# RWKV-7 layer: head sums for two blocks at a time in parts of the array's columns, low LoRA products paired over the two halves of rows

## The chip, the cores and the metric

The kernel runs on one core of one Trainium2 chip. The metric is the device time of one execution in microseconds (us). The engines are named as in the profile: PE (TensorE, matrix products; PEld is its loading of weights), DVE (VectorE), ACT (ScalarE), POOL (GpSimd) and SP (which issues most DMAs).

## The reference

A decoder trunk of two layers over 512 tokens with 1024 features, all in fp32: a recurrent RG-LRU block, then an RWKV-7 time mixing block, each followed by a gated MLP with a convolution. The change touches the RWKV-7 block only, which has 16 heads of 64 features. What matters of it:

```python
w = -jax.nn.softplus(-(w0 + jnp.tanh(xw @ w1) @ w2).astype(f32)) - 0.5      # LoRA, rank 64
decay = jnp.exp(-jnp.exp(w))
a = jax.nn.sigmoid((a0 + (xa @ a1) @ a2).astype(f32))                        # LoRA, rank 64
kk = (kf * k_k).reshape(bsz, seq, RWKV_H, RWKV_N)
kk = kk / jnp.maximum(jnp.linalg.norm(kk, axis=-1, keepdims=True), 1e-12)    # sum of squares of each head
kf = kf * (1.0 + (a - 1.0) * k_a)
y = _rwkv7_scan(rh, hs(decay), kh, vh, -kk, kk * ah)                         # recurrence over the tokens
...
bonus = jnp.sum(rh * kh * r_k, axis=-1, keepdims=True) * vh                  # a weighted sum over each head
y = (y + bonus.reshape(bsz, seq, d)).astype(x.dtype)
```

## The kernel before

**Layout and products.** Activations lie with features on the 128 partitions, in 8 blocks of 128 features by 512 tokens; a block holds two heads. A large fp32 product is made of three products of type fp32r (`mm3`, lines 51 to 53): each operand is split into a rounded part (hi) and the rest (lo), and hi x hi, lo x hi and hi x lo are summed in PSUM. PSUM has 8 banks of 128 x 512, taken with `self.bank(name)`. Products of plain fp32 tiles, such as those of lines 915 and 1294, stand in the trace as two instructions a call.

**Order of the work.** Side work is written as Python generators. `push(task, lane)` puts one in a lane, and the large projections (`project`) call `background(rate)` after every six matmuls, which advances the generators by that many `yield` steps. The framework then orders each engine's instructions, in the main by program order and by when they are ready in its own model of time, and it chooses tile buffers and semaphores; on the chip each engine takes its instructions in that fixed order.

**Stages of the RWKV-7 block** (times from the start of the profiled execution's span).

- `rwkv_lora_k`, about 586 to 617: the first half of the k projection; beside it the generator `second` makes, block by block, the decay's and a's second LoRA products. A rank-64 operand is kept as 128 rows, hi in one half and lo in the other, so that hi x (hi and lo) is one product over 128 rows (lines 840 and 848), and the lo of the weights needs a second one over 64 rows (line 841 on rows 0 to 63, line 849 on rows 64 to 127). A sigmoid on ACT follows each (843 and 850), and four scans on DVE (846) the decay's.
- `rwkv_krv`, about 617 to 700: the second half of k, and r. Beside it `prepare(g)` runs for g = 0 and 1, each over four blocks j: ACT makes exponentials and squares (`sq`, tag "tmp", two buffers), and PE sums the squares over each head with the selector `sel` into 8 rows of one bank, `ssq` (line 915, accumulated over j). After the fourth, ACT copies the 8 rows (926), PE turns them by four transposes (930) so that tokens lie on partitions, DVE takes reciprocals (932 to 934), PE turns them back (938) and spreads them over the features again (947). Then `solve(H)` (lane 1, later 2) inverts small triangular blocks: PE products (1017), 31 pairs of DVE operations (1038 and 1040), DVE transposes (1043 and 1045), PE products (1062 and 1074).
- `rwkv_chunks`, from about 700: v by tokens (lines 986 to 988), then the recurrence in 17 steps of one 64-token chunk each (`step(n)`: L1198, L1206, L1150, L1216, L1164, L1229, L1243 on PE; L1157, L1179, L1237 and L1238 on DVE), with other generators as filling. `bonus(H)`, H = 0 and 1, is one of these: DVE makes a product `pr` for each of four blocks (line 1292, tag "sq", three buffers that are shared with `ysq` and `bv` of `tail`), PE sums it over heads with the selector `selk`, which holds r_k (line 1294, accumulated into 8 rows), ACT copies (1296), PE transposes (1300), ACT copies to `bons[H]` (1301). `tail(H, c2)` normalises the output of two chunks and needs `bons[H]`; its last transposes are line 1275.

`tile_position=(row, column)` on a matmul names the corner of the part of the 128 x 128 array that it uses. The recurrence uses it throughout.

Of the kernel before, what the change touches and what calls it, by code (L numbers as in the profile page):

```python
# [7 lines left out]
F32 = mybir.dt.float32  # L8
F32R = mybir.dt.float32r
AF = mybir.ActivationFunctionType  # L10
ALU = mybir.AluOpType
# [4 lines left out]
P = 128  # L16
D = 1024
T = 512
KB = D // P
# [22 lines left out]
class Kernel:  # L42
# [647 lines left out]
    def rwkv(self):  # L690
        nc, tc = self.nc, self.tc
        x = self.x
        with tc.tile_pool(name="rbig", bufs=1) as big:

            PC = big.tile([P, KB, NC], F32, name="PC")
            selk = big.tile([P, KB, 8], F32, name="selk")

            early = [big.tile([P, 2, 2, T], F32R, tag=f"LT{i}", name=f"early{i}", bufs=1) for i in range(2)]
            again = lambda name, *shape, dt=F32: big.tile([P] + list(shape), dt, tag=name, name=name, bufs=1)
            self.LT, self.big = lambda i: again(f"LT{i}", 32, C), big  # L700

            with tc.tile_pool(name="rl", bufs=1) as pool:
                AR, BK = ([again(f"{part}{i}", 4, 4, 4 * C) for i in range(2)] for part in ("AR", "BK"))
                mk, mr = self.rwkv_lora_k(pool, AR, BK, early)
            LTs = {}
            with tc.tile_pool(name="rk", bufs=1) as pool:
                mv = self.rwkv_krv(pool, mk, mr, AR, BK, PC, selk, LTs)
            with tc.tile_pool(name="rch", bufs=1) as pool:
                return self.rwkv_chunks(pool, mv, AR, BK, PC, selk, LTs, again)
# [31 lines left out]
    @staticmethod  # L741
    def bytok(t):
        return t.rearrange("p (c q t) -> p c q t", q=2, t=C)
# [34 lines left out]
    def rwkv_lora_k(self, pool, AR, BK, early):  # L778

        nc, I = self.nc, self.I  # L780
# [13 lines left out]
        tw, ta = pool.tile([P, T], F32R, name="tw"), pool.tile([P, T], F32R, name="ta")  # L794
# [24 lines left out]
        def second():  # L819

            keep = pool.tile([P, 2, C], F32, name="keep")
            nc.vector.memset(keep, 1.0)
            nc.vector.memset(keep[:, :, 0:1], 0.0)
            kp = keep.rearrange("p q t -> p (q t)")
            ws = []
            for name, r in (("w2", 0), ("a2", 64)):
                raw = self.b4(F32, (D,), "l2raw")
                nc.sync.dma_start(raw[0:64, :], I["rwkv_" + name][0])
                nc.sync.dma_start(raw[64:128, :], I["rwkv_" + name][0])
                hi, lo = self.b4(F32R, (D,), "l2h"), self.b4(F32R, (D,), "l2l")  # L830
                nc.scalar.copy(hi, raw)
                nc.vector.tensor_tensor(lo[r : r + 64, :], raw[r : r + 64, :], hi[r : r + 64, :].bitcast(F32), ALU.subtract)
                ws.append((hi, lo))
                yield 1
            for _ in range(3):
                yield 1
            for b in range(KB):
                s = slice(b * P, (b + 1) * P)
                ps = self.bank("l2w")
                nc.tensor.matmul(ps, ws[0][0][:, s], tw, start=True, stop=False)  # L840
                nc.tensor.matmul(ps, ws[0][1][0:64, s], tw[0:64, :], start=False, stop=True)
                sg = pool.tile([P, T], F32, tag="sg", name="sg", bufs=2)
                nc.scalar.activation(sg, ps, AF.Sigmoid, bias=self.vec("rwkv_w0", b))
                yield 1
                for c in range(4):
                    nc.vector.tensor_tensor_scan(AR[b // 4][:, b % 4, c, C : 3 * C], kp, sg[:, c * P : (c + 1) * P], 0.0, ALU.mult, ALU.add)
                ps = self.bank("l2a")
                nc.tensor.matmul(ps, ws[1][0][:, s], ta, start=True, stop=False)
                nc.tensor.matmul(ps, ws[1][1][64:128, s], ta[64:128, :], start=False, stop=True)
                nc.scalar.activation(self.inner(BK, b), self.bytok(ps), AF.Sigmoid, bias=self.vec("rwkv_a0", b))  # L850
                yield 1

        self.push(second())

        mr = []
# [13 lines left out]
    def rwkv_krv(self, pool, mk, mr, AR, BK, PC, selk, LTs):  # L869

        nc = self.nc

        def t(tag, bufs):
            return pool.tile([P, T], F32, tag=tag, name=tag, bufs=bufs)


        sel = pool.tile([P, 4, 40], F32, name="sel")
        n8 = pool.tile([P, 4, 40], F32, name="n8")
        for m in (sel, selk, n8):
            nc.gpsimd.memset(m, 0.0)  # L880
        for e in range(2):
            hb = slice(e * 64, e * 64 + 64)
            for b in range(4):
                for part in (0, 32):
                    c = part + 2 * b + e
                    nc.gpsimd.memset(sel[hb, b, c : c + 1], 1.0)
            for b in range(KB):
                c = 2 * (b % 4) + e
                nc.gpsimd.tensor_copy(selk[hb, b, c : c + 1], self.vec("rwkv_r_k", b)[hb])
        psb = self.bank("back")  # L890
        for j in range(4):
            nc.tensor.transpose(psb[0:40, j * P : (j + 1) * P], sel[:, j, :], self.ident)
# [7 lines left out]
        def prepare(g):  # L900


            ssq = self.bank("ssq")
            for j in range(4):
                b = g * 4 + j
                pad = ppads[b % 2]
                pp = pad.rearrange("p (c q) t -> p c q t", q=2)
                Lc, rr, a, ko = self.inner(AR, b), self.outer(AR, b), self.inner(BK, b), self.outer(BK, b)
                sq, pinv, fac, kp = t("tmp", 2), t("pinv", 2), t("fac", 1), t("kp", 1)
                nc.scalar.activation(bytok(pinv), Lc, AF.Exp, scale=DECAY_C)  # L910
                nc.scalar.activation(bytok(sq), ko, AF.Square, scale=self.vec("rwkv_k_k", b))
                nc.scalar.activation(bytok(fac), a, AF.Identity, bias=self.oka[:, b : b + 1], scale=self.vec("rwkv_k_a", b))
                nc.scalar.activation(pp[:, :, :, 1:], Lc, AF.Exp, scale=-DECAY_C)
                yield 1
                nc.tensor.matmul(ssq[0:8, :], sel[:, j, 0:8], sq, start=j == 0, stop=j == 3)  # L915
                nc.vector.tensor_tensor(bytok(kp), ko, bytok(pinv), ALU.mult)
                nc.vector.scalar_tensor_tensor(a, a, self.vec("rwkv_k_k", b), bytok(kp), ALU.mult, ALU.mult)
                yield 1
                (nc.vector.tensor_copy if g else nc.scalar.copy)(rr, pp[:, :, :, 1:])
                self.done.add(("r", b))  # L920
                nc.vector.tensor_tensor(Lc, ko, pp[:, :, :, 0:C], ALU.mult)
                nc.vector.tensor_tensor(ko, bytok(kp), bytok(fac), ALU.mult)
                nc.scalar.copy(PC[:, b, :], pad[:, :, C])
                yield 1
            ss = t("tmp", 2)[0:8]
            nc.scalar.copy(ss, ssq[0:8])
            yield 1
            pt = self.bank("sst")
            for c in range(4):
                nc.tensor.transpose(pt[:, c * 8 : c * 8 + 8], ss[:, c * P : (c + 1) * P], self.ident[0:8, 0:8])  # L930
            pv = pt[:, 0:32].rearrange("p (c h) -> p c h", h=8)
            nc.vector.tensor_scalar(n8[:, :, 0:8], pv, 1e-24, None, ALU.max)
            for part in (32, 0):
                nc.vector.reciprocal(n8[:, :, part : part + 8], n8[:, :, 0:8])
            yield 1
            pr = self.bank("rec")
# [6 lines left out]
            for j in range(4):  # L943
                b = g * 4 + j
# [137 lines left out]
    def rwkv_chunks(self, pool, mv, AR, BK, PC, selk, LTs, again):  # L1082
# [9 lines left out]
        nc, tc, I = self.nc, self.tc, self.I  # L1092
# [21 lines left out]
        bons = [pool.tile([P, 4, 8], F32, name=f"bon{i}") for i in range(2)]  # L1114
# [171 lines left out]
        def bonus(H):  # L1286

            pn = self.bank("bon")
            for i in range(4):
                b = H * 4 + i  # L1290
                pr = self.xsp.tile([P, T], F32, tag="sq", name="pr", bufs=3)
                nc.vector.tensor_tensor(self.bytok(pr), self.outer(AR, b), self.outer(BK, b), ALU.mult)
                yield 1
                nc.tensor.matmul(pn[0:8, :], selk[:, b, :], pr, start=i == 0, stop=i == 3)
            bt = self.xsp.tile([P, T], F32, tag="sq", name="bt", bufs=3)
            nc.scalar.copy(bt[0:8, :], pn[0:8, :])
            yield 1
            pt = self.bank("bont")
            for c in range(4):
                nc.tensor.transpose(pt[:, c * 8 : c * 8 + 8], bt[0:8, c * P : (c + 1) * P], self.ident[0:8, 0:8])  # L1300
            nc.scalar.copy(bons[H], pt[:, 0:32].rearrange("p (c h) -> p c h", h=8))
            self.done.add(("bonus", H))
            yield 1

# [199 lines left out]
```

## Time and profile before

| | |
|---|---|
| runs | 1363.87, 1361.54, 1357.82 us; median 1361.54 |
| profiled execution | 1359.88 us, span of its instructions 1357.9 us |
| granted PE clock, mean | 0.989 |
| PE, PEld busy | 1324.4 us, 1068.8 us |
| DVE, ACT, POOL busy | 863.6, 632.6, 68.8 us |
| DMA | 120.20 MB, mean 89 GB/s |

Busy time of PE is the union of its matmuls' durations, whose ends are modelled: matmuls overlap, so the distance between starts tells more of a matmul's cost than its duration does. In the rows, `128*8` is the part of the array (rows by columns) and `128x512` the data that is streamed; "x16" counts instructions. L12 is line 12 of the kernel before. "Idle before" is time in which the engine did nothing ahead of the instruction, with what released it.

### The profile page before, as it was taken

To read this page: it belongs to the slowest core of one execution; us is meant where nothing else is said; L and a number is where in the kernel's file an instruction comes from. 1 tells how busy PE (TensorE), PEld (TensorE's weight loads), DVE (VectorE), ACT (ScalarE), POOL (GpSimd) and SP (SyncE) were. 2 spreads that over 40 slices of the span, in tenths; PEclk is the share of its full clock that TensorE was granted. 3 is DMA by queue.
4 is the path that set the end of the run, shared out by engine and by line. 5 is a ranking of instruction groups with operands and counts; after the bars stand their busy time and mean duration, and the time that the engine had idled before them with its cause. 6 is when DMAs were issued, how large, how long until landed. Compare 5 with 4: busy or idle time off the path is not lost.

```text
span 1357.9 us, 19301 instructions
## 1 busy us (share of the span) xinstructions
PE 1324.4 (98%) x7827; PEld 1068.8 (79%) x7827; DVE 863.6 (64%) x1332; ACT 632.6 (47%) x1032; POOL 68.8 (5%) x113
## 2 busy tenths in 40 slices
PE   8999999999999999999999988898999999999998
PEld 7877888888888888866679776676888888888886
DVE  5988756555354755597897975776646464365623
ACT  6797534333233523378636578653634242244311
POOL 4000000000000000020011011110000000000000
PEclk8999999999999999999999989998999999999999
DMA  5423333232333434222121111212333222334311
GB/s 182 119 62 93 109 94 109 79 104 67 106 94 94 143 93 125 63 72 79 62 86 49 58 33 64 56 60 65 109 93 94 77 93 78 109 94 126 122 63 62
DMA packets 72120, 120.20 MB, mean 89 GB/s; under 512 B 9498, under 2 KB 21476, under 8 KB 71904
## 3 DMA queue, kind: packets, MB, share of 16 engines
q1 hardware_dynamic: 70672, 117.20, 27.9%
q8 instruction: 61, 1.00, 0.3%
q10 hardware_dynamic: 576, 1.05, 0.2%
q0 software_dynamic: 784, 0.74, 0.2%
q14 instruction: 27, 0.22, 0.1%
HBM read 114.44 MB, written 4.52 MB: 88 GB/s over the span
## 4 chain that ended last, share of the span: by engine, by line
PE 89%; DVE 6%; ACT 2%; issue 1%; DMA 1%; POOL 1%; SPq 0%; POOLq 0%; ACTq 0%; DVEq 0%
PE acc L51 22%; PE acc L53 22%; PE acc L52 22%; PE acc L616 3%; PE acc L615 3%; PE acc L617 3%; PE acc L986 1%; PE s L1150 1%; PE pe L1198 1%; PE acc L987 1%; PE py L1206 1%; PE acc L988 1%; DVE W L1157 1%; PE ssq L915 1%; DMA xin<-in_x_dram 1%
## 5 line engine op out<-in xcount | busy, mean ns | idle before, releaser
L51 PE MATMUL acc<-xs,wh 128*128 128x512 f32 x896 | 352.1, 393 | 0.0
L53 PE MATMUL acc<-xs,wl 128*128 128x512 f32 x896 | 349.0, 390 | 0.7 <-DVE wl L91 0.7
L52 PE MATMUL acc<-xs,wh 128*128 128x512 f32 x896 | 349.5, 390 | 0.0
L91 DVE TENSOR_TENSOR wl<-raw,wh 128x1024 fp32r<-128x1024 f32 (+1 forms) x201 | 242.6, 1215 | 164.6 <-PE acc L52 90.1
L90 ACT CAST wh<-raw 128x1024 fp32r<-128x1024 f32 (+1 forms) x201 | 208.1, 1045 | 258.6 <-DVE wl L91 167.6
L53 PEld LDWEIGHTS acc<-xs,wl 128*128 128x128 f32 x896 | 168.5, 188 | 36.5 <-DVE wl L91 1.2
L51 PEld LDWEIGHTS acc<-xs,wh 128*128 128x128 f32 x896 | 168.8, 188 | 35.0 <-ACT wh L90 0.2
L52 PEld LDWEIGHTS acc<-xs,wh 128*128 128x128 f32 x896 | 168.7, 188 | 34.7 <-DVE wl L91 0.2
L576 DVE SCALAR_TENSOR_TENSOR cv<-gpad,pv,cv 128x512 f32<-128x512 f32 x96 | 71.8, 748 | 22.6 <-ACT cv L574 21.5
L90 ACT CAST hid<-un 128x512 fp32r<-128x512 f32 x48 | 29.8, 620 | 109.2 <-DVE un L583 109.1
L616 PE MATMUL acc<-wh,hid 128*128 128x512 f32 (+1 forms) x200 | 76.8, 384 | 0.0
L615 PE MATMUL acc<-wh,hid 128*128 128x512 f32 (+1 forms) x200 | 76.5, 382 | 0.0
L617 PE MATMUL acc<-wl,hid 128*128 128x512 f32 (+1 forms) x200 | 75.9, 380 | 0.0
L52 PE MATMUL acc<-hid,wh 128*128 128x512 f32 x192 | 75.7, 394 | 0.0
L53 PE MATMUL acc<-hid,wl 128*128 128x512 f32 x192 | 75.6, 394 | 0.0
L51 PE MATMUL acc<-hid,wh 128*128 128x512 f32 x192 | 75.5, 393 | 0.0
L582 DVE TENSOR_TENSOR un<-acc,rb 128x512 f32<-128x512 f32 x48 | 33.0, 688 | 43.5 <-PE acc L53 43.5
L91 DVE TENSOR_TENSOR hid<-un,hid 128x512 fp32r<-128x512 f32 x48 | 33.1, 690 | 32.0 <-ACT hid L90 32.0
L574 ACT ACTIVATE cv<-gpad,pv 128x512 f32<-128x512 f32 x48 | 39.2, 817 | 20.1 <-DVE gpad L571 19.9
L578 ACT ACTIVATE ge<-cv 128x512 f32<-128x512 f32 x48 | 30.1, 627 | 35.9 <-DVE cv L576 35.9
L620 DVE TENSOR_TENSOR xtok<-xtok,acc 128x512 f32<-128x512 f32 (+1 forms) x25 | 16.6, 665 | 45.6 <-PE acc L617 45.6
L615 PEld LDWEIGHTS acc<-wh,hid 128*128 128x128 f32 x200 | 37.5, 188 | 8.0
(424 smaller groups left out, 2207.6 us busy)
## 6 DMA issues: line engine op xcount, KB each, us to landing
raw<-in_ffn_w_up_dram SPq DMA_DIRECT2D x96, 512.0 KB, 3.9
raw<-in_ffn_w_down_dram SPq DMA_DIRECT2D x48, 512.0 KB, 3.8
raw<-in_rwkv_w_rkv_dram SPq DMA_DIRECT2D x24, 512.0 KB, 3.8
raw<-in_lru_w_in_dram SPq DMA_DIRECT2D x16, 512.0 KB, 3.9
raw<-in_lru_w_out_dram SPq DMA_DIRECT2D x8, 512.0 KB, 3.7
raw<-in_rwkv_w_out_dram SPq DMA_DIRECT2D x8, 512.0 KB, 3.5
xd<-x SPq DMA_DIRECT2D x8, 256.0 KB, 2.0
AR<-xd SPq DMA_DIRECT2D x1, 2048.0 KB, 8.8
```

What stands on the lines that cost most here:

```text
L51: nc.tensor.matmul(ps, wh, xh, start=start, stop=False)
L52: nc.tensor.matmul(ps, wh, xl, start=False, stop=False)
L53: nc.tensor.matmul(ps, wl, xh, start=False, stop=stop)
L90: (self.nc.vector.tensor_copy if dve else self.nc.scalar.copy)(hi, src)
L91: self.nc.vector.tensor_tensor(lo, src, hi.bitcast(F32), ALU.subtract)
L574: nc.scalar.activation(cv, gp[:, 0:T], AF.Identity, bias=self.vec(f"ffn_conv_b{l}", fb), scale=cw(0))
L576: nc.vector.scalar_tensor_tensor(cv, gp[:, j : j + T], cw(j), cv, ALU.mult, ALU.add)
L578: nc.scalar.activation(ges[o], cv, AF.Gelu_apprx_tanh)
L582: nc.vector.tensor_tensor(un, ps, rbs[0], ALU.mult)
L615: nc.tensor.matmul(ps, hh[:, s], wh[:, k, m], start=kk == 0, stop=False)
L616: nc.tensor.matmul(ps, hl[:, s], wh[:, k, m], start=False, stop=False)
L617: nc.tensor.matmul(ps, hh[:, s], wl[:, k, m], start=False, stop=kk == 7)
```

## The change

1. **Low LoRA products.** In `second`, each block takes two banks, `pw` and `pa`, at once. The two products over 128 rows come first, then, after a `yield`, the two products over 64 rows next to each other, with `tile_position` (0, 0) and (64, 0); both sigmoids and the scans follow them in the same step. The number of steps, products, sigmoids and scans is the same.
2. **Sums of squares.** In `prepare`, the squares of blocks j = 0 and 1 (then 2 and 3) are kept until both are there, and are then summed by two products next to each other, each into 32 rows of the bank at 32 j, `tile_position` (0, 32 j), not accumulated. The selector is the same 32 columns of `sel` for every block. The copy takes 128 rows instead of 8, the transposes are 128 x 128 instead of 8 x 128, and DVE reads columns 0 and 1 of each strip of 32.
3. **Bonus.** The same in `bonus`: two products `pr` are kept, then summed by a pair of products in strips of 32 columns; copy, transposes and the last copy change likewise. `selk` has 32 columns a block instead of 8.

```diff
-            selk = big.tile([P, KB, 8], F32, name="selk")
+            selk = big.tile([P, KB, 32], F32, name="selk")
...
             for b in range(KB):
                 s = slice(b * P, (b + 1) * P)
-                ps = self.bank("l2w")
-                nc.tensor.matmul(ps, ws[0][0][:, s], tw, start=True, stop=False)
-                nc.tensor.matmul(ps, ws[0][1][0:64, s], tw[0:64, :], start=False, stop=True)
+                pw, pa = self.bank("l2w"), self.bank("l2a")
+                nc.tensor.matmul(pw, ws[0][0][:, s], tw, start=True, stop=False)
+                nc.tensor.matmul(pa, ws[1][0][:, s], ta, start=True, stop=False)
+                yield 1
+
+                nc.tensor.matmul(pw, ws[0][1][0:64, s], tw[0:64, :], start=False, stop=True, tile_position=(0, 0))
+                nc.tensor.matmul(pa, ws[1][1][64:128, s], ta[64:128, :], start=False, stop=True, tile_position=(64, 0))
                 sg = pool.tile([P, T], F32, tag="sg", name="sg", bufs=2)
-                nc.scalar.activation(sg, ps, AF.Sigmoid, bias=self.vec("rwkv_w0", b))
-                yield 1
+                nc.scalar.activation(sg, pw, AF.Sigmoid, bias=self.vec("rwkv_w0", b))
                 for c in range(4):
                     nc.vector.tensor_tensor_scan(AR[b // 4][:, b % 4, c, C : 3 * C], kp, sg[:, c * P : (c + 1) * P], 0.0, ALU.mult, ALU.add)
-                ps = self.bank("l2a")
-                nc.tensor.matmul(ps, ws[1][0][:, s], ta, start=True, stop=False)
-                nc.tensor.matmul(ps, ws[1][1][64:128, s], ta[64:128, :], start=False, stop=True)
-                nc.scalar.activation(self.inner(BK, b), self.bytok(ps), AF.Sigmoid, bias=self.vec("rwkv_a0", b))
+                nc.scalar.activation(self.inner(BK, b), self.bytok(pa), AF.Sigmoid, bias=self.vec("rwkv_a0", b))
                 yield 1
...
             for b in range(KB):
-                c = 2 * (b % 4) + e
-                nc.gpsimd.tensor_copy(selk[hb, b, c : c + 1], self.vec("rwkv_r_k", b)[hb])
+                nc.gpsimd.tensor_copy(selk[hb, b, e : e + 1], self.vec("rwkv_r_k", b)[hb])
...
             ssq = self.bank("ssq")
+            sqs = []
...
-                nc.tensor.matmul(ssq[0:8, :], sel[:, j, 0:8], sq, start=j == 0, stop=j == 3)
+                sqs.append(sq)
+                for i in (j - 1, j) if j % 2 else ():
+                    nc.tensor.matmul(ssq[32 * i : 32 * i + 32, :], sel[:, 0, 0:32], sqs[i], start=True, stop=True, tile_position=(0, 32 * i))
...
-            ss = t("tmp", 2)[0:8]
-            nc.scalar.copy(ss, ssq[0:8])
+            ss = t("tmp", 2)
+            nc.scalar.copy(ss, ssq)
             yield 1
             pt = self.bank("sst")
             for c in range(4):
-                nc.tensor.transpose(pt[:, c * 8 : c * 8 + 8], ss[:, c * P : (c + 1) * P], self.ident[0:8, 0:8])
-            pv = pt[:, 0:32].rearrange("p (c h) -> p c h", h=8)
-            nc.vector.tensor_scalar(n8[:, :, 0:8], pv, 1e-24, None, ALU.max)
+                nc.tensor.transpose(pt[:, c * P : (c + 1) * P], ss[:, c * P : (c + 1) * P], self.ident)
+            pv = pt.rearrange("p (c j w) -> p c j w", c=4, w=32)[:, :, :, 0:2]
+            nc.vector.tensor_scalar(n8[:, :, 0:8].rearrange("p c (j e) -> p c j e", e=2), pv, 1e-24, None, ALU.max)
...
             pn = self.bank("bon")
+            prs = []
             for i in range(4):
                 b = H * 4 + i
                 pr = self.xsp.tile([P, T], F32, tag="sq", name="pr", bufs=3)
                 nc.vector.tensor_tensor(self.bytok(pr), self.outer(AR, b), self.outer(BK, b), ALU.mult)
+                prs.append(pr)
                 yield 1
-                nc.tensor.matmul(pn[0:8, :], selk[:, b, :], pr, start=i == 0, stop=i == 3)
+
+                for j in (i - 1, i) if i % 2 else ():
+                    nc.tensor.matmul(pn[32 * j : 32 * j + 32, :], selk[:, H * 4 + j, :], prs[j], start=True, stop=True, tile_position=(0, 32 * j))
             bt = self.xsp.tile([P, T], F32, tag="sq", name="bt", bufs=3)
-            nc.scalar.copy(bt[0:8, :], pn[0:8, :])
+            nc.scalar.copy(bt, pn)
             yield 1
             pt = self.bank("bont")
             for c in range(4):
-                nc.tensor.transpose(pt[:, c * 8 : c * 8 + 8], bt[0:8, c * P : (c + 1) * P], self.ident[0:8, 0:8])
-            nc.scalar.copy(bons[H], pt[:, 0:32].rearrange("p (c h) -> p c h", h=8))
+                nc.tensor.transpose(pt[:, c * P : (c + 1) * P], bt[:, c * P : (c + 1) * P], self.ident)
+            nc.scalar.copy(bons[H].rearrange("p c (j e) -> p c j e", e=2), pt.rearrange("p (c j w) -> p c j w", c=4, w=32)[:, :, :, 0:2])
```

## The prediction, made before the changed kernel was run

> **What bounds the kernel now.** I read the page first, then the busy time by stage, then PE's waits, and then the order of PE's instructions around every line the change touches.
>
> ```profile
> PE 1324.4 (98%) x7827; PEld 1068.8 (79%) x7827; DVE 863.6 (64%) x1332; ACT 632.6 (47%) x1032; POOL 68.8 (5%) x113
> ...
> PE 89%; DVE 6%; ACT 2%; issue 1%; DMA 1%; POOL 1%; SPq 0%; POOLq 0%; ACTq 0%; DVEq 0%
> ```
>
> PE carries 89% of the chain that ended last, so a microsecond of PE time counts wherever PE does not wait. The stages in which the changed lines run (times from the span's start) are these:
>
> ```profile
> core 0: us, PE busy (x) PEld busy (x) DVE busy (x) ACT busy (x) POOL busy (x), PEclk, DMA share, GB/s
> 599.40:617.30 17.90, 17.90 (x59) 9.65 (x57) 13.12 (x34) 12.85 (x20) 0.04 (x1) 1.00 0.34 106
> 617.00:651.00 34.00, 34.00 (x141) 23.38 (x141) 27.46 (x47) 31.86 (x57) 1.04 (x18) 1.00 0.26 78
> 673.60:729.50 55.90, 55.90 (x377) 44.10 (x376) 54.11 (x113) 20.74 (x41) 4.33 (x15) 1.00 0.23 71
> 740.00:786.00 46.00, 42.12 (x623) 34.40 (x622) 43.23 (x101) 29.94 (x72) 5.88 (x5) 1.00 0.18 55
> 786.00:840.00 54.00, 49.49 (x836) 40.21 (x836) 34.47 (x60) 39.17 (x99) 6.60 (x6) 0.91 0.09 27
> ```
>
> In the first three rows PE is busy for the whole stretch. A busy PE may still run with bubbles, which is what this change is about, but it is not waiting for anybody. But the neighbours are close behind: ACT works 31.86 of 34.00 us in the second row, DVE 54.11 of 55.90 us in the third. In the fourth row PE does wait and DVE, at 43.23 of 46.00 us, sets the pace.
>
> **Low LoRA products.** Each of 8 blocks has two of them, over 64 rows of the array (L841, L849). PE start times show what leaving and re-entering the full array costs:
>
> ```profile
> 593.86 0.39 PE L52 MATMUL acc<-mix,wh 128*128 128x512 f32 x1
> 594.08 0.39 PE L53 MATMUL acc<-mix,wl 128*128 128x512 f32 x1
> 594.40 0.49 PE L841 MATMUL l2w<-tw,l2l 64*128 64x512 f32 x1
> 594.82 0.50 PE L51 MATMUL acc<-mix,wh 128*128 128x512 f32 x1
> 595.16 0.40 PE L52 MATMUL acc<-mix,wh 128*128 128x512 f32 x1
> ```
>
> A full matmul starts about 0.23 us after the one before. From L53 (594.08) to the second full one after L841 (595.16) it is 1.08 us where two ordinary steps would be 0.46: one "trip" to a 64-row product costs 0.62 us, though the product alone is worth 0.23. Once the trace already has two such products, on different halves of the rows, side by side:
>
> ```profile
> 600.84 0.39 PE L840 MATMUL l2w<-tw,l2h 128*128 128x512 f32 x1
> 601.15 0.50 PE L849 MATMUL l2a<-ta,l2l 64*128 64x512 f32 x1
> 601.16 0.49 PE L841 MATMUL l2w<-tw,l2l 64*128 64x512 f32 x1
> ...
> 602.15 0.40 PE L848 MATMUL l2a<-ta,l2h 128*128 128x512 f32 x1
> ```
> ```profile
> L841 PE MATMUL l2w<-tw,l2l 64*128 64x512 f32 x8 | 4.0, 495 | 0.0
> L849 PE MATMUL l2a<-ta,l2l 64*128 64x512 f32 x8 | 3.7, 481 | 0.0
> ```
>
> They start 0.01 us apart, so the second is free. That one trip holds three products and takes 602.15 - 600.84 - 0.46 = 0.85 us; the other 13 of the 16 go alone. Before: 13 x 0.62 + 0.85 = 8.9 us. After: eight trips, 5.0 us. I expect block 0 to stay split, because the first L841 runs at 594.40 and the first L849 only at 601.15: 9 trips, 5.6 us, **a gain of 3.3 us**. The ends: 3.9 us gained if all eight pair up, and 16 x 0.62 - 8.9 = 1.0 us lost if none does. I take the upper part, as the two lines now stand next to each other and become ready together.
>
> The full products move ahead of both low ones and hold two banks at once (pw, pa), and the sigmoids, the scan and L850 come in one step. Number, length and engine of those stay; the cover is PE's project matmuls, which go on between the steps. ACT has 5.0 us and DVE 4.8 us left in 599.40 to 617.30, so both fit in a stretch that is 3.3 us shorter; where they don't, a bank comes free late (second rival).
>
> **Sums of squares.** L915 is an fp32 product with 8 columns, and each call runs as two passes (x2):
>
> ```profile
> 625.54 0.39 PE L53 MATMUL acc<-mix,wl 128*128 128x512 f32 x1
> 625.86 1.02 PE L915 MATMUL ssq<-tmp,sel 128*8 128x512 f32 x2
> 626.81 0.50 PE L51 MATMUL acc<-mix,wh 128*128 128x512 f32 x1
> 627.15 0.39 PE L52 MATMUL acc<-mix,wh 128*128 128x512 f32 x1
> ```
> One call costs 627.15 - 625.54 - 0.46 = 1.15 us, eight 9.2 us. After, two calls stand in different 32-column strips and go as a pair. What a pair costs no row shows for 512 columns of data; for 64 there is a close one, fp32 in two passes on the two column halves (L1198):
>
> ```profile
> 744.23 0.68 PE L1198 MATMUL pe<-sv,W 128*64 128x64 f32 x8
> 744.84 0.32 PE L1206 MATMUL py<-sv,rts 64*64 64x64 f32 x2
> ...
> 748.63 1.02 PE L1294 MATMUL bon<-pr,selk 128*8 128x512 f32 x2
> 749.59 0.39 PE L986 MATMUL acc<-wh,mix 128*128 128x256 f32 x1
> ...
> 753.02 0.69 PE L1198 MATMUL pe<-sv,W 128*64 128x64 f32 x16
> 753.63 0.27 PE L1206 MATMUL py<-sv,AR 64*64 64x64 f32 x1
> ```
>
> Eight passes on one half take 0.61 us to the next line (744.23 to 744.84), sixteen on both halves also 0.61 us (753.02 to 753.63): the second half is free. So a pair costs one trip, 1.15 us: four pairs, 4.6 us, **a gain of 4.6 us**. The ends: 4.6, and, with no overlap, two passes more for each pair. Two passes with the exit behind them hold up the follower 0.96 us (748.63 to 749.59); the exit is about what 0.42 (594.40 to 594.82) is over 0.32 (594.08 to 594.40), 0.1, so two passes are 0.86: a gain of 0.29 a pair, 1.2 us in all. I take the upper end, as L1198 is the same kind of pair.
>
> The Trainium skill speaks against this: TensorE: Matmul & The Clock Gate, section "The mechanism", says that a weight load overlaps running matmuls only where its row group differs, and that matmuls start strictly in order; column strips share their rows. L1198's 16 passes in the time of 8 disagree with it so far, at 64 columns of data. What it would give here is the first rival.
>
> Waits that this adds: the pair waits for the later square, so a "tmp" buffer (2 of them) is held one block longer, and the next L911 on ACT can be late. ACT has 2.1 us idle between 617 and 651, so one late square is free there; if more are late, the project's casts of weights behind them on ACT are late too, and the second rival has the price.
>
> **Transposes and copies.** L930 and L1300 become full 128-wide transposes like L938:
>
> ```profile
> L938 PE MATMUL rec<-ident,n 128*40 128x128 f32 x8 | 1.2, 271 | 0.0
> ...
> L930 PE MATMUL sst<-ident,tmp 8*128 8x8 f32 x8 | 0.8, 207 | 0.0
> ```
>
> Sixteen of them at 64 ns more are 1.0 us lost at most; against that each of the four groups need no longer leave the full array (0.62 us a trip above, less if the neighbours are narrow too). Between 1.0 lost and 2.5 gained I take 0.2 us gained, near zero, as both effects are seen in the rows and are of like size. Copies over 128 partitions instead of 8 have the same 512 columns; the larger clearing of selk is on POOL, busy 5%: nothing for both, and if POOL were late the first bonus product, over 100 us later, is the cover.
>
> **Bonus.** The row of L1294 gives its instructions with the first and the last start:
>
> ```profile
> L1294 PE MATMUL bon<-pr,selk x16: 592/594/597, 748.6 to 833.5; 128*8 128x512 f32 x16
> ```
>
> Each call delays its follower 0.96 us, as above. Bonus(0), the first half, lies from 748.6 on in the fourth stage, where DVE sets the pace: the two calls saved (1.9 us) only lengthen PE's next wait, so nothing. Bonus(1), which ends the row, lies in the fifth stage and is partly on the chain; PE is busy 49.49 of 54.00 us there. Two calls saved are 1.9 us at most, 0 at least; I take half, **1.0 us**.
>
> **The sum.** 3.3 + 4.6 + 0.2 + 1.0 = 9.1 us. The profiled execution took 1359.88 us (span 1357.9), so 1350.8 by its measure; it stood 1.66 us under the median of the three runs, 1361.54. For a median I forecast **1352.4 us**.
>
> **Rivals.** *Column strips overlap partly or not.* With no overlap squares give 1.2 and bonus(1) 0.1: 3.3 + 1.2 + 0.2 + 0.1 = 4.8, 1356.7 us, chance 0.05. If the second product's first pass starts only with the first one's second pass, each pair pays half of 0.86: squares 2.9, bonus 0.5, sum 6.9, 1354.6 us, chance 0.07. For both: no row shows 512 columns in strips. Against both: L1198.
>
> The second figure, 1354.6 us, is the one that the Trainium skill's rule on row groups and order, cited above, would give.
>
> *The chain of ACT and DVE is the next bound.* PE's lead must be matched by prepare(0) and the solve.
>
> ```profile
> 727.37 2.08 DVE L1045 STREAM_TRANSPOSE XN<-X 128x1024 f32<-128x1024 f32 x1
> ```
> ```profile
> 731.46 0.69 PE L1062 MATMUL m1p<-XN,O 32*32 32x32 f32 x32
> ```
> ```profile
> PE pz L1275 <- DVE ytok L1271: 10.8, 4, 3.8
> ```
>
> PE uses XN 2.0 us after DVE ends it (729.45 to 731.46), after a stretch in which DVE has 1.8 us idle of 55.9. If ACT can draw in only its 2.1 us of idle time between 617 and 651, PE keeps 2.1 + 2.0 and bonus(1)'s 1.0: 5.1 us, 1356.4 us. Against: ACT's work there can slip to later, and from 673.6 on it works only 20.74 of 55.90 us. Chance 0.21.
>
> *Slower.* Products pr are now held from one step to the next, in 3 buffers shared with the tails' ysq and bv. If DVE stands in its queue for such a buffer, the state updates (L1237, L1238) behind it wait, and PE for those. The price of such a wait is at most that of the longest that PE has for DVE's tail, 3.8 us; four pairs 15.2 us, less the 8.1 us before the bonus: 1368.6 us. It decides from 8.1 + 6.8 = 14.9 us on. Against: PE's waits, of which the longest row stands above, name no product pr now. Chance 0.07.
>
> **How the numbers follow.** Within 0.5% means 1354.7 to 1368.3 us, about what can be told from no change here. The forecast has 0.55 (its own range 1348 to 1355.5), a larger gain with bonus(0) kept as well (1349) 0.05, the rivals 0.12, 0.21 and 0.07. Faster takes 0.50 + 0.05 and a few hundredths of each of the first two rivals: 0.62; slower 0.08 with a reshuffled order counted in; same 0.30. The range goes from 3.9 + 4.6 + 0.2 + 1.9 + 1.9 = 12.5 us of gain and 3 us of scatter (runs 1357.82 to 1363.87), 1346, to the two slow rivals and some scatter, 1359.
>
> **What would show it.** Right: L841 and L849 starting within 0.01 us in at least 7 places; both L915 of a pair starting together, and the next full matmul no later than after one; PE without waits up to 740; a longer PE wait near 763 or 786. Wrong: the second strip starting 0.4 us or more behind, a PE wait for XN, or DVE idle ahead of L1292.

## The result, and the profile after

| | median us | runs | ratio to before |
|---|---|---|---|
| before | 1363.87 (1357.82 to 1366.32) | 13 | |
| after | 1355.47 (1352.75 to 1358.58) | 13 | 0.9939 [0.9927, 0.9951] |

The medians differ by 8.4 us; the ratio gives 0.6%, 8.3 us (6.7 to 10.0 by its interval). The forecast was 9.1 us of gain and 1352.4 us. Of the 3.1 us between forecast and median, 2.3 are the median of before, which was 1361.54 over three runs; the gain itself is 0.7 us short. That is not because the terms were right: three of the five were wrong, in both directions, and their errors partly cancelled, which is luck. The median also stands at the very edge of the forecast's own range (1348 to 1355.5).

The profiled executions show less than the medians: 1359.88 us before, 1356.4 after, 3.5 us. In these two, stretches at half clock are 3.4 or 6.8 us long and lie at different places, and the mean granted clock differs from run to run (0.983 to 0.992 in the runs of after). Over the runs of the fourteen kernels of this study, without one run of before at 1860.1 us and a mean granted clock of 0.654, one line fits: 0.73 us less for each 0.001 more of mean granted clock, about which the runs of a kernel scatter by 1.1 us (standard deviation). The experiments' table therefore has a column "at equal clock" (mean granted clock 0.988), good to about 0.3 us for 12 runs and 0.5 for 6; before itself reads 1361.1 to 1361.7 in it on the four chips used. At equal clock before takes 1361.5 us and after 1356.0: 5.4 us (differences are taken before rounding). The rest of the medians' difference goes with the clock, which is partly the kernel's own doing, as bonus(1) shows below. By this measure the sum of the second rival, 5.1 us, is nearer than the forecast's 9.1.

From the page of the changed kernel, PE's and the others' busy time, and the shares of the chain that ended last:

```profile
PE 1318.6 (97%) x7827; PEld 1070.2 (79%) x7827; DVE 861.7 (64%) x1332; ACT 631.9 (47%) x1032; POOL 68.4 (5%) x113
...
PE 86%; DVE 7%; ACT 4%; issue 2%; POOL 1%; DMA 1%; SPq 0%; POOLq 0%; ACTq 0%; DVEq 0%
```

PE is busy 5.8 us less (1324.4 to 1318.6) and has 3 points less of the chain; DVE and ACT have 3 more. PE's waits in the changed kernel (who waits for what: us in total, times, longest; pz are the tail's transposes, m1p the product of solve that reads DVE's transpose XN, acc at L989 the products of v, knb the products that spread the reciprocals rec over the features; the changed kernel's lines stand up to 7 further down than those of before):

```profile
PE pz L1278 <- DVE ytok L1274: 7.6, 3, 3.8
...
PE m1p L1065 <- DVE XN L1048: 2.9, 1, 2.9
PE bon L1301 <- DVE pr L1296: 2.8, 1, 2.8
...
PE acc L989 <- DVE X L1043: 2.2, 1, 2.2
...
PE knb L950 <- DVE rec L944: 1.2, 1, 1.2
```

Of four waits for DVE's tail (10.8 us before) three are left, but the first has not vanished: PE now waits 2.2 us ahead of L989 at 778.14, right before the first pz, where it waited 3.2 us for ytok. The rows for knb and for the bonus product are new too; the experiments show where they come from.

**Low LoRA products.** PE's timeline of the changed kernel (start, duration, engine, line, operation):

```profile
600.47 0.50 PE L840 MATMUL l2w<-tw,l2h 128*128 128x512 f32 x1
600.90 0.49 PE L845 MATMUL l2a<-ta,l2l 64*128 64x512 f32 x1
600.90 0.50 PE L844 MATMUL l2w<-tw,l2l 64*128 64x512 f32 x1
601.23 0.39 PE L845 MATMUL l2a<-ta,l2l 64*128 64x512 f32 x1
...
602.23 0.50 PE L845 MATMUL l2a<-ta,l2l 64*128 64x512 f32 x1
...
608.15 0.49 PE L844 MATMUL l2w<-tw,l2l 64*128 64x512 f32 x1
608.15 0.50 PE L845 MATMUL l2a<-ta,l2l 64*128 64x512 f32 x1
608.58 0.50 PE L840 MATMUL l2w<-tw,l2h 128*128 128x512 f32 x1
```

At 608.15 a pair starts as one. But at 600.90 the L845 of one block meets the L844 of another, and at 602.23 an L845 stands alone. Three clean pairs, one group of three and seven products alone make eleven trips, not the nine of the forecast: the two lines stand together in the code, but not in the order in which they were issued.

**Sums of squares.** The first pair of prepare(0), and the second (L918 is L915 of before):

```profile
627.49 0.39 PE L53 MATMUL acc<-mix,wl 128*128 128x512 f32 x1
627.81 1.05 PE L918 MATMUL ssq<-tmp,sel 128*32 128x512 f32 x4
628.79 0.50 PE L51 MATMUL acc<-mix,wh 128*128 128x512 f32 x1
629.13 0.39 PE L52 MATMUL acc<-mix,wh 128*128 128x512 f32 x1
```
```profile
633.56 1.04 PE L918 MATMUL ssq<-tmp,sel 128*32 128x512 f32 x2
634.53 0.50 PE L51 MATMUL acc<-mix,wh 128*128 128x512 f32 x1
...
636.58 1.05 PE L918 MATMUL ssq<-tmp,sel 128*32 128x512 f32 x2
```

Four passes (x4) take from 627.49 to 629.13, less two ordinary steps 1.18 us; one call took 1.15 before. The second strip is free. But the second pair of prepare(0) was drawn apart: two calls, 3.02 us from each other, each at the price of a pair.

**Bonus(0).** The forecast put nothing down here. Before, at the end of the stage (DVE, POOL, PE):

```profile
777.99 2.02 DVE L1043 STREAM_TRANSPOSE LT<-X 128x1024 f32<-128x1024 f32 x1
...
783.32 1.51 DVE L1270 TENSOR_TENSOR ytok<-ytok,lnw 128x512 f32<-128x512 f32 x1
...
785.09 0.68 DVE L1271 TENSOR_TENSOR ytok<-ytok,bv 128x512 f32<-128x512 f32 x1
...
783.25 1.04 POOL L1263 TENSOR_TENSOR bv<-x,bon 128x512 f32<-128x512 f32 x1
785.92 0.87 PE L1275 MATMUL pz<-ident,ytok 128*128 128x128 f32 x3 [3.19 <-DVE ytok L1271]
```

After:

```profile
776.39 0.69 DVE L1273 TENSOR_TENSOR ytok<-ytok,lnw 128x512 f32<-128x512 f32 x1
...
777.33 0.68 DVE L1274 TENSOR_TENSOR ytok<-ytok,bv 128x512 f32<-128x512 f32 x1
777.93 0.18 DVE L1043 TENSOR_TENSOR X<-X,DA 128x31 f32<-128x31 f32 x1
778.14 1.98 DVE L1046 STREAM_TRANSPOSE LT<-X 128x1024 f32<-128x1024 f32 x1
...
778.48 0.97 PE L1278 MATMUL pz<-ident,ytok 128*128 128x128 f32 x4
```

Before, the transpose of 2.02 us stood in DVE's queue ahead of the tail's last steps, and L1270 took 1.51 us beside POOL's bv. After, the transpose stands behind them, and the same step takes 0.69 us. 2.02 + 0.82 = 2.8 us earlier, about what the stage was shortened by (from the second transpose to A to the first pz: 785.92 - 739.59 = 46.33 us before, 778.48 - 735.08 = 43.40 after). The same holds in all the kernels below: this stretch takes 46.3 to 47.3 us in the five whose bonus is that of before (before, e1, e2, e4, e6) and 43.4 to 43.7 us in the nine with pairs in bonus(0). That DVE's order is the cause is read from the traces; no run moves the transpose alone.

**Bonus(1).** Its first pair and what became of its second:

```profile
818.67 1.05 PE L1301 MATMUL bon<-pr,selk 128*32 128x512 f32 x4
...
823.01 0.69 DVE L1272 TENSOR_TENSOR ytok<-ytok,mu 128x512 f32<-128x512 f32 x1 [1.16 <-POOL mu L1269]
823.62 0.68 DVE L1296 TENSOR_TENSOR pr<-AR,BK 128x512 f32<-128x512 f32 x1
...
824.36 1.92 PE L1301 MATMUL bon<-pr,selk 128*32 128x512 f32 x2 [2.82 <-DVE pr L1296]
824.82 0.68 DVE L1296 TENSOR_TENSOR pr<-AR,BK 128x512 f32<-128x512 f32 x1
```
```profile
822.90:829.70 6.80, 5.34 (x28) 2.15 (x28) 3.94 (x7) 3.12 (x8) 1.42 (x3) 0.50 0.00 0
```

DVE waits 1.16 us for POOL's mu of a tail, and pr is behind it; PE, whose order has the bonus product next, waits 2.82 us, and the clock is granted at half for 6.8 us (the windows' row: 0.50). The third and fourth product go alone after all, 1.92 and 1.85 us each. From the first pz of the second tail to that of the third, PE took 834.00 - 811.39 = 22.61 us before and 829.89 - 804.22 = 25.67 after: 3.1 us lost. Half clock is a part of it: 5.2 us of that stretch ran at half before and 10.2 us after.

### The profile page after: what moved, and what is told of

Read it like the earlier page. It is cut to its first block, busy times and chain, and to the rows that moved or that the text cites. A ratio compares the mean times of both kernels' runs of the same rounds, so it can differ in the third digit from the quotient of the medians.

```text
span 1354.3 us, 19293 instructions
## 1 busy us (share of the span) xinstructions
PE 1318.6 (97%) x7827; PEld 1070.2 (79%) x7827; DVE 861.7 (64%) x1332; ACT 631.9 (47%) x1032; POOL 68.4 (5%) x113
## 4 chain that ended last, share of the span: by engine, by line
PE 86%; DVE 7%; ACT 4%; issue 2%; POOL 1%; DMA 1%; SPq 0%; POOLq 0%; ACTq 0%; DVEq 0%
PE acc L51 22%; PE acc L53 22%; PE acc L52 22%; PE acc L616 3%; PE acc L615 3%; PE acc L617 3%; PE acc L989 1%; DVE W L1160 1%; DVE X L1043 1%; DVE DA L1041 1%; PE acc L991 1%; PE pe L1201 1%; PE acc L990 1%; POOL mu L1269 1%; PE s L1153 1%
## 5 line engine op out<-in xcount | busy, mean ns | idle before, releaser
L51 PE MATMUL acc<-xs,wh 128*128 128x512 f32 x896 | 351.8, 393 | 0.0
L51 PEld LDWEIGHTS acc<-xs,wh 128*128 128x128 f32 x896 | 168.8, 188 | 35.0 <-ACT wh L90 0.2
L51 PE MATMUL acc<-hid,wh 128*128 128x512 f32 x192 | 75.5, 393 | 0.0
```

The source lines that it names most:

```text
L51: nc.tensor.matmul(ps, wh, xh, start=start, stop=False)
```

## The experiments

Each kernel is timed beside before on the same chip; the letters of the theories mean what each expectation says. The ratios' intervals are about 0.2% wide to each side: they don't tell e1 and e6 from before, nor e5, e7, e8 and e10 to e12 from after. What is said of those rests on the times at equal clock and on the traces. "Lead" is how much earlier than before PE or DVE starts a step in the profiled execution, both traces laid on the same first cast of LoRA weights (L831 of before): LoRA over (PE's transposes to `back`), solve(0) begins (DVE's transpose to A), solve(1) begins, and the first and the third pz of the tails. The last column also holds that execution's own half-clock stretches.

| kernel | median (runs), us | ratio to before | at equal clock | LoRA over | solve(0) | solve(1) | pz 1 | pz 3 |
|---|---|---|---|---|---|---|---|---|
| before | (85 in all) | | 1361.5 | | | | | |
| after | 1355.47 (13) | 0.9939 [0.9927, 0.9951] | 1356.0 | 1.96 | 3.15 | 4.35 | 7.27 | 3.95 |
| e1_lora | 1359.54 (12) | 0.9983 [0.9964, 1.0001] | 1359.3 | 1.86 | 1.88 | 1.88 | 0.99 | 3.65 |
| e2_ssq | 1356.88 (12) | 0.9963 [0.9945, 0.998] | 1357.2 | 0.00 | 2.85 | 4.05 | 3.13 | 3.10 |
| e3_bonus | 1359.03 (12) | 0.9975 [0.9961, 0.9989] | 1359.7 | 0.11 | 0.11 | 0.12 | 3.06 | -0.97 |
| e4_lora_ssq | 1357.96 (12) | 0.9974 [0.9959, 0.9989] | 1357.6 | 1.85 | 3.03 | 4.22 | 3.32 | 0.36 |
| e5_pin | 1351.26 (6) | 0.9934 [0.9911, 0.9957] | 1352.7 | 3.87 | 5.73 | 6.93 | 9.84 | 6.55 |
| e6_ssq_nostrip | 1359.68 (12) | 0.9987 [0.997, 1.0005] | 1360.4 | 0.00 | 1.76 | 1.03 | 0.12 | -3.79 |
| e7_relief | 1353.14 (9) | 0.9942 [0.9925, 0.996] | 1353.8 | 1.96 | 4.69 | 5.88 | 8.81 | 4.78 |
| e8_bon0 | 1352.79 (6) | 0.9941 [0.9919, 0.9962] | 1353.8 | 1.96 | 3.12 | 4.31 | 7.09 | 8.26 |
| e9_ssqtie | 1356.95 (12) | 0.9969 [0.9953, 0.9985] | 1356.8 | 1.96 | 1.74 | 2.94 | 5.87 | 5.07 |
| e10_best | 1352.97 (6) | 0.9938 [0.9916, 0.9961] | 1352.4 | 3.87 | 2.79 | 3.98 | 6.90 | 7.28 |
| e11_best_relief | 1354.25 (9) | 0.9953 [0.9934, 0.9972] | 1354.0 | 3.84 | 0.45 | 1.64 | 4.55 | 4.94 |
| e12_fin | 1350.42 (6) | 0.991 [0.9888, 0.9931] | 1351.7 | 3.87 | 3.55 | 4.75 | 7.43 | 8.60 |

**One part at a time.** e1 to e4 are before with the diff's LoRA hunk alone, prepare's hunk alone, the bonus hunks alone, and the first two together.

> The paired low LoRA products alone. Theory A (the trace of the changed kernel: only three of eight pairs stand alone side by side and one shares a trip with a third product, PE is 1.75 us ahead of before at 615): 1.5 to 2 us faster than before, the low products again in about 11 trips off the full array, and no more than that behind 700. Theory B (the prediction's sum): 3.3 us faster. Theory C (a changed order moves the later stages by chance): anything from 4 us faster to 4 us slower, with PE waits between 735 and 930 that differ by more than 2 us.

> The sums of squares in column strips alone. Theory A: a pair costs PE one trip of 1.16 us (second pass 0.45 us after the first); of four pairs at least three stay together, 3.5 to 4.6 us less on PE up to 700, of which a wait for the reciprocals (1.2 us in the changed kernel) may take back some: 2.5 to 4.5 us faster. Theory B: 4.6 us faster, all of it kept. Theory C: as for the LoRA kernel, anything within 4 us of zero through the later stages.

> The bonus in column strips alone; up to 700 the kernel is that of before. Theory A (the changed kernel's trace: bonus(0) shortens the stage around 750 by 2 us and more, bonus(1) makes PE wait 2.8 us for its products, after which the clock of PE is low): between 2 us faster and 2 us slower. Theory B: 1.0 us faster, from bonus(1). Theory C, the other extreme: the 3.4 us by which the medians differ more than the two profiled executions come from here: 3 to 4 us faster.

> The change without its bonus part. Theory A: the sum of the two parts before it, 4.5 to 6 us faster than before; if bonus(1) costs more than bonus(0) brings, it beats the whole change (8.4 us by the medians) or comes near it. Theory B: 7.9 us faster. Theory C: the parts do not add up, by more than 2 us.

At equal clock LoRA gives 2.2 us, the squares 4.3, the bonus 1.8; together 8.3, but after gives 5.4. Already e4 gives only 3.9 where e1 and e2 add up to 6.5, and its trace shows where: at the start of solve(0) it leads by 3.03 us, e2 alone by 2.85. LoRA's 1.9 us are there when prepare(0) begins and gone when it ends. In e4, as in after, the second pair of squares is drawn apart (L919 there, at 632.76 and 635.78), which costs PE a trip more (0.97 us); in e2 it stands together. The rest of the lead ends in PE's wait for rec (1.17 us in e4, 0.30 in e2): DVE begins rec 57.7 us behind the first cast in e4 and 57.5 us in e2, no earlier. e3's lead jumps by 2.9 us between solve(1) and the first pz: bonus(0) gains. It is lost by the third pz, but 20.5 us of that way ran at half clock, and e6 (below), whose bonus is that of before, loses 3.9 us there with a half-clock stretch as long. That bonus(1) loses is shown by e8, not by e3's trace.

**The LoRA pairs tied.** Both 64-row products of a block are kept in the program's order:

```diff
-nc.tensor.matmul(pw, ws[0][1][0:64, s], ...)
-nc.tensor.matmul(pa, ws[1][1][64:128, s], ...)
+tc.keep_in_program_order(nc.tensor.matmul(pw, ws[0][1][0:64, s], ...))
+tc.keep_in_program_order(nc.tensor.matmul(pa, ws[1][1][64:128, s], ...))
```

> The changed kernel with the two 64-row products of a block tied together in the order of the program, so that up to 8 pairs stand side by side instead of the 4 of now (about 11 trips). Theory A (a trip saved is worth its 0.62 us to the end): 3 trips less, 1.9 us, 1353.6 us. Theory B (what the LoRA stage gives is taken back by the chain of ACT and DVE in prepare(0)): no change, 1355.0 to 1356.0 us; PE starts the first sums-of-squares product earlier by up to 1.9 us, and its wait ahead of the first knb product (L950) for DVE's rec (L944) grows from 1.2 us by about as much.

Now eight trips: six pairs, one group of three, one alone. A pair, and the waits left:

```profile
602.22 0.50 PE L844 MATMUL l2w<-tw,l2l 64*128 64x512 f32 x1
602.23 0.49 PE L845 MATMUL l2a<-ta,l2l 64*128 64x512 f32 x1
602.65 0.50 PE L52 MATMUL acc<-mix,wh 128*128 128x512 f32 x1
```
```profile
PE knb L950 <- DVE rec L944: 0.5, 1, 0.5
```

The lead after LoRA is 3.87 us; eight trips, one of them of three products, should give 8.9 - 7 x 0.62 - 0.85 = 3.7. So the price of a trip holds. The lead goes on to solve(0), and the wait for rec falls to 0.5 us instead of growing: that prepare(0) takes all that LoRA gives is refuted for this order. It grows to 5.73, 2.6 more than after's, as DVE begins rec 2.6 us earlier (55.05 us behind the first cast; 57.63 in after). Why ACT and DVE come to it sooner in the order of e5 is not shown; the calls of prepare(0) moved too. At equal clock e5 is 3.3 us under after.

**Two squares in a row, without strips.** Against before:

```diff
-nc.tensor.matmul(ssq[0:8, :], sel[:, j, 0:8], sq, start=j == 0, stop=j == 3)
+sqs.append(sq)
+for i in (j - 1, j) if j % 2 else ():
+    nc.tensor.matmul(ssq[0:8, :], sel[:, i, 0:8], sqs[i], start=i == 0, stop=i == 3)
```

> The kernel before with one edit: two of the sums of squares are issued one behind the other, in the same 8 columns and one accumulation, without strips. To be compared with e2_ssq (1356.9 us), which has the strips. Theory A (the strips' overlap carries the gain): a pair spares only its exit and entry, 0.29 us, 1.2 us in all: 1361.0 to 1362.0 us, and a pair of calls holds its follower up about 1.9 us, against 1.0 to 1.1 in e2_ssq. Rival (it is enough to leave the full array once for two): 1357 to 1358.5 us.

```profile
630.48 1.88 PE L918 MATMUL ssq<-tmp,sel 128*8 128x512 f32 x4
632.30 0.50 PE L51 MATMUL acc<-mix,wh 128*128 128x512 f32 x1
```

The follower comes 1.82 us behind the pair; in strips it was 0.98. The lead when solve(1) begins is 1.03 us against e2's 4.05. The strips carry the gain, not the standing together.

**ACT relieved in prepare(0).** Against after, for g = 0 the copies rr and PC go to POOL:

```diff
-(nc.vector.tensor_copy if g else nc.scalar.copy)(rr, pp[:, :, :, 1:])
+(nc.vector if g else nc.gpsimd).tensor_copy(rr, pp[:, :, :, 1:])
-nc.scalar.copy(PC[:, b, :], pad[:, :, C])
+(nc.scalar.copy if g else nc.gpsimd.tensor_copy)(PC[:, b, :], pad[:, :, C])
```

> The changed kernel with the eight copies of prepare(0) that ACT makes (rr L922 and PC L926, 4 x 0.62 and 4 x 0.2 us) given to POOL. Theory B (prepare(0) is held by ACT and DVE, and eats PE's lead): the wait of 1.2 us ahead of knb goes, DVE begins the transpose to A 1 to 2.5 us earlier (L1027 or its neighbour), total 1353.0 to 1354.5 us. Theory A (PE alone bounds that stretch): no change, 1355.0 to 1356.0 us. Should the copies on POOL hold up DVE, slower by 1 us or more.

The fourth square on ACT and the second pair on PE, in after (its pair is shown above) and in e7:

```profile
633.78 0.72 ACT L911 ACTIVATE tmp<-BK,pv 128x512 f32<-128x512 f32 x1
```
```profile
630.16 0.71 ACT L911 ACTIVATE tmp<-BK,pv 128x512 f32<-128x512 f32 x1
...
632.90 1.05 PE L918 MATMUL ssq<-tmp,sel 128*32 128x512 f32 x4
```

Both measured from the first cast, which is 0.66 us earlier in e7, the square comes 3.0 us earlier; the pair stands together, DVE begins rec 1.6 us earlier, PE's wait for rec falls to 0.3 us, and solve(0) begins 1.5 us earlier than in after. At equal clock e7 is 2.3 us under after. Two things changed at once, though, ACT's load and the pair; e9 was to tell them apart.

**Bonus(1) one by one**, each product in its strip; bonus(0) stays in pairs. Against after:

```diff
-for j in (i - 1, i) if i % 2 else ():
+for j in (i,) if H else (i - 1, i) if i % 2 else ():
```

> The changed kernel with the products of bonus(1) issued one by one as before, each into its strip; bonus(0) stays in pairs. Theory C (holding back the first product of a pair is what costs 3 us in bonus(1): PE's wait of 2.8 us for pr L1296, and the half clock behind it): the wait goes, 1352.5 to 1353.5 us. Rival (the pairs of bonus(1) are worth their two trips, 1.9 us, and the wait only takes the place of a later one at pz): 1355.5 to 1357.5 us.

```profile
816.00:830.00 14.00, 13.49 (x228) 9.32 (x221) 10.34 (x20) 12.09 (x33) 3.91 (x4) 1.00 0.10 23
```

PE is busy 13.49 of 14.00 us at full clock where after waited and ran at half. From the second tail's first pz to the third's it takes 825.22 - 804.10 = 21.12 us, 3.4 of them at half clock. The wait for pr is gone (in the five kernels with pairs in bonus(1) it is 0.5 to 2.8 us, and in the nine others there is none), the third pz leads by 8.26 us instead of 3.95, at equal clock e8 is 2.2 us under after, and its six runs lie within 1.8 us (1352.0 to 1353.8) where after's thirteen spread over 5.8. In bonus(1) the pairs cost more than their two trips are worth.

**The squares tied**, against after (the two L918 of a pair kept in the program's order, as in e5):

> The changed kernel with the two sums of squares of a pair tied together in the order of the program; ACT's work stays as it is. In the changed kernel the second pair of prepare(0) was drawn apart (L918 at 633.56 and 636.58), in e7_relief it stood together. Theory D (the drawn-apart pair is what LoRA's gain was lost on, and what e7 gave back): two passes and one trip less, 1.1 us, and the wait of 1.2 us ahead of knb goes: 1353.0 to 1354.5 us, as e7. Theory B (it is ACT's load): no change or a longer wait at knb, 1355.0 to 1356.5 us, since the pair now waits for the later square.

```profile
634.15 0.72 ACT L911 ACTIVATE tmp<-BK,pv 128x512 f32<-128x512 f32 x1
...
641.13 1.05 PE L918 MATMUL ssq<-tmp,sel 128*32 128x512 f32 x4
```
```profile
PE knb L950 <- DVE rec L944: 1.9, 1, 1.9
...
649.80:653.20 3.40, 3.40 (x16) 2.04 (x18) 3.40 (x5) 2.67 (x6) 0.00 (x0) 0.50 0.07 27
```

Theory D fails: e9 is 0.7 us over after at equal clock, and the longer wait of theory B is there. The pair stands together, but PE's order now has it at 641.13, 6.3 us after its last square was done. Even so DVE begins rec no later than in after: 57.55 us behind the first cast, 57.63 there. What PE saves on the pair it waits longer for rec (1.9 us, 1.2 in after), and a stretch of 3.4 us at half clock follows. The loss lies there: from the first knb to solve(0) it takes 21.8 us in after, e4, e5, e7 and e8, and 23.3 in e9. So neither the drawn-apart pair nor the time of the last sum is what holds rec back in after. There (PE, DVE):

```profile
639.04 0.60 PE L933 MATMUL sst<-ident,tmp 128*128 128x128 f32 x4
...
639.74 1.23 DVE L91 TENSOR_TENSOR wl<-raw,wh 128x1024 fp32r<-128x1024 f32 x1 [1.33 <-ACT wh L90]
...
642.15 0.18 DVE L935 TENSOR_SCALAR n<-sst 128x32 f32<-128x32 f32 x1
...
647.82 0.68 DVE L944 TENSOR_TENSOR rec<-rec 8x512 fp32r<-8x512 f32 x1
```

The transposed sums are there at 639.64, but DVE takes the max (L935) at 642.15, behind three other steps, the first of which waited 1.33 us for ACT. In after, then, the order and load of DVE and ACT set rec (in e9 DVE waits 0.7 us for the late sums and catches up). Where no half clock follows, solve(0) moves with rec: in e5 and e7 rec begins 2.6 and 1.6 us earlier than in after, and solve(0) 2.6 and 1.5.

**The edits together**: e10 is e5, e8 and e9; e11 adds e7; e12 is e5, e7 and e8 without the tied squares.

> The edits of e5 (LoRA pairs tied), e9 (squares tied) and e8 (bonus(1) one by one) together. If each is PE time or a wait of its own, the gains add: about 3 us from e5, 2 to 3 us from e8, and up to 1.5 us from e9: 1348.5 to 1350.5 us. Theory B (they share one limit in prepare(0) and in DVE's tail): not better than e5 alone, 1351 to 1353 us.

> e10 with the eight copies of prepare(0) on POOL as in e7. Theory D (the order was all that e7 gave): the same as e10 within 0.7 us. Theory B (with PE 2 to 3 us earlier, ACT's load in prepare(0) binds again): 1 us or more under e10, and no wait of PE ahead of knb, where e10 has one.

> LoRA pairs tied (e5), prepare(0)'s eight copies on POOL (e7), bonus(1) one by one (e8); the squares stay untied, and stand in pairs in the order of the program by themselves. Theory B (ACT's queue in prepare(0) sets when the last square, and so rec and knb, are there): the gains of e5, e7 and e8 add in part, PE waits for rec less than 1 us ahead of knb: 1348 to 1350 us. Theory E (e5's gain and e7's are the same microseconds): as e5 with bonus(1) changed, 1350 to 1352 us.

e10 and e11 fall short where e9 did: their lead sinks from 3.87 and 3.84 us to 2.79 and 0.45 across prepare(0), PE waits 1.7 and 1.9 us for rec, and 3.4 and 6.8 us at half clock follow. With the tie taken out (e12) the pair starts at 630.83, 0.83 us behind its square:

```profile
629.28 0.72 ACT L911 ACTIVATE tmp<-BK,pv 128x512 f32<-128x512 f32 x1
...
630.83 1.05 PE L918 MATMUL ssq<-tmp,sel 128*32 128x512 f32 x4
```
```profile
PE knb L950 <- DVE rec L944: 2.1, 1, 2.1
```

and yet PE waits 2.1 us for rec, as DVE and ACT take the steps behind the squares (max, reciprocals, rec) no earlier than in e5: rec begins 55.46 us behind the first cast, 55.05 there. Here too 3.4 us at half clock follow. e12 has the lowest median, 1350.42 us, 0.991 [0.9888, 0.9931] of before, and so is faster than before and, at equal clock, 4.4 us under after; but its 1351.7 there is not told apart from e10's 1352.4 or e5's 1352.7. e5's and e7's gains are largely the same microseconds.

## Why the prediction came out as it did

- **Low LoRA products, 3.3 us: the size was wrong, 1.9 to 2.0 us** when the stage ends (e1, after). The step that failed is "nine trips". Its ground was that the lines stand next to each other and become ready together; the order of issue still interleaved two blocks, and there were eleven. The price of 0.62 us held: 8.9 less ten trips at 0.62 and one of three products at 0.85 gives 1.9, and in e5, with eight trips, the upper end of 3.9 was reached. "L841 and L849 starting within 0.01 us in at least 7 places" was the right sign to name; there were four.
- **Squares, 4.6 us: right where PE sets the pace.** e2's PE starts its first product of v (L986 of before) 4.59 us earlier. It keeps 3.1 by the first pz: the stretch from solve(1) to there takes 0.9 us longer in e1, e2, e4 and e6 than in before; why is not shown. The first rival falls: the second strip starts 0.006 us after the first, and e6 without strips leads by 1.02 us at the same product, where the forecast's lower end was 1.2. The Trainium skill's sentence (TensorE: Matmul & The Clock Gate, "The mechanism") that weight loads overlap running matmuls only where the row group differs was read by the prediction as making the second strip half late; at 512 columns, as at L1198's 64, this trace disagrees with that reading.
- **Transposes, 0.2 us:** not measured apart. Their effect lies within the 4.59 us of e2.
- **Bonus(0), 0 us: wrong, 2.9 us gained** (e3: lead 0.12 to 3.06). The step was "the two calls saved only lengthen PE's next wait". DVE sets the pace there, as said, but its order changed: the 2 us transpose of solve(1) fell behind the tail instead of ahead of it, and one step no longer ran beside POOL's. The sign "a longer PE wait near 763 or 786" did not come: the wait there fell from 3.2 to 2.2 us.
- **Bonus(1), 1.0 us gained: the direction was wrong, 2.2 us lost** by e8 at equal clock, about 3 in the trace with its half clock (22.61 to 25.67 us). It is the mechanism of the "slower" rival with another link. pr did not stand in the queue for a buffer, but behind a tail step that waited for POOL; a pair held back then makes PE wait for the later product. The sign "DVE idle ahead of L1292" came in this form (1.16 us). The argument that PE's waits named no product pr was worth little: before, each product was used as it came.
- **The second rival** (ACT and DVE the next bound) holds in part. PE does wait for rec, 1.2 us, where the forecast had "PE without waits up to 740", and in after and e4 a part of LoRA's lead ends in that wait. ACT's 2.1 us of idle time was not the bound, though: e7, with less work on ACT, is 2.3 us faster at equal clock, and in e5 rec itself begins 2.6 us earlier. PE's wait for XN, named as a sign against, was there before already, in solve(1) at 810.40, and grew from 2.5 to 2.9 us: the forecast had read solve(0) alone, where PE waits for XN in neither kernel.

Open: which steps of ACT and DVE bring rec forward in e5 and e7; no run changes the order of these two engines by itself. And how much of the difference between 8.4 us of the medians and 5.4 us at equal clock belongs to waits that the change removes: only the profiled executions have a trace.

## What to carry to other kernels

Price a saved trip from PE start times, then count in the issued order how many trips are really saved: lines that stand together in the code are not together on the engine until they are tied, and a tie puts them where the program has them, which in e9 was 6.3 us after their operands were ready. Pairing two products makes the first wait for the second, which is free where the operands are long there and dear where they come from a queue that is just in time: bonus(0) and bonus(1) are the same code. Where another engine sets the pace, look at its order, not only at its sum.

## What the runs showed of the hardware

- Half clock comes in stretches of 3.4 us and multiples (3.4, 6.8, 10.2, 20.5 in the profiled executions), and in each of the 14 executions all changes of the granted clock lie on one grid of 3.41 us. Between 560 and 960 us PE has 62 waits of 1.7 to 3.8 us in these traces (not counting one of 1.9 us at L51 that stands 2 to 3 us behind a wait for pz). In 58 cases a half-clock stretch began during the wait or within 2.3 us of its end; the other four are a wait of 2.5 us for XN in e1 and waits of 2.2 us ahead of acc in e3, e7 and e9. Of the waits of 1.0 to 1.4 us none was followed by one. So the length alone doesn't decide it; whether the place on the grid does was not tested.
- The same DVE step took 1.51 us beside POOL's bv and 0.69 without it. That alone is 0.8 us of the stage. It holds in all 14 traces: 1.50 to 1.52 us in the five in which the first tail's step ran beside bv, 0.69 in the nine others. Not every step is slowed: W<-s,masks took 0.69 us beside bv in before (at 767.34).
- Two fp32 products of 512 columns in different strips of 32 columns start 0.006 us apart and hold up what follows by 0.98 us, as one alone does (0.97 us); two in the same columns by 1.82 us.
